# 64-column products in a delta-rule inversion on one Trainium2 core, with S5's skip moved from TensorE to VectorE

## The chip, the cores and the metric

The kernel runs on one core of a Trainium2 chip. The metric is the device time of one execution in microseconds (us). The core's engines work from queues of their own: TensorE (PE in the profile; its weight loads are PEld), VectorE (DVE), ScalarE (ACT), GpSimd (POOL) and SyncE (SP, which here issues most of the DMAs). All share the on-chip memory SBUF; TensorE writes its results to PSUM.

## The reference

A decoder trunk of two layers on 1024 positions with 1024 channels, all in f32. Each layer runs a token mixer beside a cross-attention into 256 memory tokens, projects both together, and ends with an MLP. The first layer's mixer is a gated delta rule with 8 heads of 128 channels in chunks, the second's is an S5 state-space layer. What matters here:

```python
def gated_delta_rule_chunked(q, k, v, g, beta):
    ...
    a_strict = jnp.where(strict, jnp.einsum('bhnid,bhnjd->bhnij', kb, k) * decay, 0.0)
    rhs = jnp.concatenate([vb, kb * jnp.exp(gc)[..., None]], axis=-1)
    sol = lax.linalg.triangular_solve(eye + a_strict, rhs, left_side=True, lower=True,
                                      unit_diagonal=True)
    ...

def s5_mixer(...):
    ...
    y = s5_scan(u, abar_re, abar_im, bbar_re, bbar_im, c_re, c_im)
    y = y + d_skip * u                         # the skip
    zg = jax.nn.gelu(y)
    out = zg * jax.nn.sigmoid(zg @ w_glu + b_glu)

for i in range(2):
    h = jnp.concatenate([mix, cross], axis=-1) @ w_o[i]
    x = layer_norm(DN_ALPHA * x + h, ln1_g[i], ln1_b[i])
    f = jnp.square(jax.nn.relu(x @ mlp_w1[i])) @ mlp_w2[i]
    x = layer_norm(DN_ALPHA * x + f, ln2_g[i], ln2_b[i])
```

## The kernel before

**Matmuls.** The large products split each f32 operand into a rounded high part and a rest in the type f32r, and add three products of 128x128 by 128x512 (`mm3`, L364 to L366). Small products are in plain f32; each of them appears on TensorE as two loads of weights and two matmul instructions. In a product the stationary operand (the first) is loaded as weights, the moving one (the second) streams past.

**The delta rule.** The kernel uses chunks of 128 positions, so a head has 8 tiles of 128x128, handled in two halves of four tiles. With N the negated strict part of a tile, it needs the inverse of I - N, transposed. It comes in steps. `gdn_keys_out` makes N^T of a half (tile `n`), writes its 32x32 diagonal blocks to DRAM (`ntd`), and then, in the kernel before, two masked copies of it (`ntf`): the blocks beside the diagonal at distance 32, and those at distance 64, each in a tile cleared by GpSimd, filled by ScalarE (L1040 to L1043) and written by a DMA that GpSimd issues. `gdn_inverse` inverts the 32x32 blocks of two heads at a time on VectorE and writes them to DRAM (`t32`, both ways round). `gdn_invert_tiles` grows them to 128x128 with five products of four tiles per half, all 128x128 by 128x128 on block-diagonal tiles in the kernel before. Every product goes to the one PSUM bank of the tag `pi`; VectorE adds the identity after two of the products (L1148), ScalarE copies the other three (L1153). That makes 8 heads x 2 halves x 5 = 80 products of four tiles. The 32x32 blocks are loaded by SyncE into two tiles that persist (`bds`), four loads for each; every other tile of the chain is a fresh one of the tag `h4` (six buffers) or, for the result, `h3` (seven).

`gdn_recur` is the recurrence over the eight tiles of a head and reads the results (`TT`). The order of the program is woven from generators: `gdn_fill` mixes the next head's projections with its inversion products, and `weave` mixes those with the recurrence of the head before.

**S5's matrices.** Beside the first MLP, `s5_side` makes the matrices of the second layer's mixer. `s5_mats`, called 16 times, has a group of four products `pz` of 128x16 by 128x128 (L1726). After each stands a product of 16x16 by 16x16 (L1727) which adds the skip: the identity times `dd`, a diagonal matrix of the skip's weights that VectorE makes (L1830). ScalarE copies the result to `z` (L1729), and GpSimd issues its DMA to DRAM (L1730).

**The order.** After the first weights are split, `settle` orders all instructions anew. It lists the instructions with their dependencies and buffers, gives each a price in us (`price`), and simulates the five engines, GpSimd's and SyncE's queues among them. TensorE takes its instructions roughly in the program's order (it may reach 40 us ahead), the other engines by the time at which TensorE will need their result, up to 70 us ahead. The order that comes out is fixed in the program; at run time each engine works through its own queue.

Of the kernel before, what the change touches and what calls it, by code (L numbers as in the profile page):

```python
# [10 lines left out]
F32 = mybir.dt.float32  # L11
F32R = mybir.dt.float32r
AF = mybir.ActivationFunctionType
ALU = mybir.AluOpType
AX = mybir.AxisListType

P = 128
# [13 lines left out]
class Trunk:  # L31
# [244 lines left out]
    def price(self, i, big):  # L276

        E = mybir.EngineType
        if i.opcode == "DMACopy":
# [8 lines left out]
            q = [x.bass_ap.ap for x in (i.ins[0], i.outs[0])]  # L288
# [3 lines left out]
        if i.engine == E.PE:  # L292
            if i.ins[0].dtype == F32R:
                return 0.014 + 0.416e-3 * big, 0.39 if big > 256 else 0.29, 0
            return (0.11, 0.27, 0) if i.is_transpose else (0.222, 0.39, 0)
        q = [x.bass_ap.ap[-1] for l in (i.ins, i.outs) for x in l if getattr(x, "bass_ap", None) is not None]
        slow = 1.65 if any(s > 1 and c > 1 for s, c in q) else 1.0
        scalars = any(math.prod(c for s, c in x.bass_ap.ap[1:]) == 1 for x in i.ins if getattr(x, "bass_ap", None) is not None) and big > 1
        if i.engine == E.Activation:
            bank = self.home.get(i.ins[0].bass_ap.tensor.name, "s")[0] == "ps"  # L300
            if i.opcode == "TensorCopy":
                t = (0.05 if bank else 0.096) + 0.84e-3 * big * slow
            else:
                t = (0.08 if bank else 0.125) + 0.8e-3 * big + (0.08 if len(i.outs) > 1 else 0.0) + (0.07 if scalars else 0.0)
            return t, t + 0.1, 0
        if i.engine == E.Pool:
            t = 0.02 + 0.87e-3 * big if i.opcode == "Memset" else 0.5 if big < 2 else 1.0 if big < 8 else 0.17 + 2.1e-3 * big
            return t, t + 0.05, 0
        wide = sum(c > 1 for x in i.ins if getattr(x, "bass_ap", None) is not None for c in [math.prod(c for s, c in x.bass_ap.ap[1:])])
# [507 lines left out]
    def gdn_consts(self):  # L817
        nc = self.nc
# [14 lines left out]
        self.early = [early[:, 2 * P + 64 * n:2 * P + 64 * (n + 1)].rearrange("p (t h) -> p t h", t=8) for n in range(2)]  # L833
        self.bds = [self.tile("h4", [P, 4, P], F32, "bd") for _ in range(2)]
        for o in self.bds:
            nc.gpsimd.memset(o, 0.0)
        cw = scr[:, P + 8 + 13 * 64:].rearrange("p (m j) -> p m j", j=4)
        nc.sync.dma_start(cw, self.a["cw"])
# [6 lines left out]
        self.ded = self.dp.tile([8, 2, P, 4, P], F32, tag="ded", name="ded")  # L845
        self.ntf = self.dp.tile([8, 2, 2, P, 4, P], F32, tag="ntf", name="ntf")
        self.ntd = self.dp.tile([8, 8, 4, 32, 32], F32, tag="ntd", name="ntd")
# [150 lines left out]
    def gdn_keys_out(self, h, hf):  # L998


        nc = self.nc
        V = nc.vector
# [34 lines left out]
        nc.gpsimd.dma_start(self.ntd[h, t4].rearrange("t b j i -> (b j) t i"), pkd)  # L1037
        for w, q in enumerate((32, 64)):
            nm = self.tile("h1", [P, 4, P], F32, "nm")
            nc.gpsimd.memset(nm, 0.0)  # L1040
            for b in range(0, P, 2 * q):
                nc.scalar.copy(nm[b:b + q, :, b + q:b + 2 * q], n[b:b + q, :, b + q:b + 2 * q])
            nc.gpsimd.dma_start(self.ntf[h, hf, w], nm)  # L1043

# [81 lines left out]

    def block_diag(self, h, hf, w):

        o = self.bds[w]
        for b in range(4):  # L1130
            q = slice(32 * b, 32 * b + 32)
            self.nc.sync.dma_start(o[q, :, q], self.t32[w, h, 4 * hf:4 * hf + 4, b].rearrange("t i c -> i t c"))
        return o

    def gdn_invert_tiles(self, h):

        nc = self.nc
        idb = self.ident.unsqueeze(1).to_broadcast([P, 4, P])

        def mm4(a, b):  # L1140
            ps = self.psum("pi", "iv", (P, 4, P))
            for t in range(4):
                nc.tensor.matmul(ps[:, t, :], a[:, t, :], b[:, t, :], start=True, stop=True)  # L1143
            return ps

        def plus_i(ps):
            o = self.tile("h4", [P, 4, P], F32, "zi")
            nc.vector.tensor_tensor(o, ps, idb, op=ALU.add)  # L1148
            return o

        def keep(ps, tag):
            o = self.tile(tag, [P, 4, P], F32, "iv")
            nc.scalar.copy(o, ps)  # L1153
            return o

        def masked(hf, w):
            o = self.tile("h4", [P, 4, P], F32, "nm")
            nc.sync.dma_start(o, self.ntf[h, hf, w])
            return o

        out = self.TT[h] = []
        for hf in range(2):
            nm = masked(hf, 0)
            T32, V32 = self.block_diag(h, hf, 0), self.block_diag(h, hf, 1)
            zi = plus_i(mm4(nm, T32))
            yield 0.8
            T64 = keep(mm4(V32, zi), "h4")
            yield 0.8
            V64 = keep(mm4(zi, V32), "h4")
            nm = masked(hf, 1)  # L1170
            yield 0.8
            zi = plus_i(mm4(nm, T64))
            yield 0.8
            out.append(keep(mm4(zi, V64), "h3"))
            yield 0.8

# [535 lines left out]
    def s5_mats(self, m, b, co, banks):  # L1712
# [12 lines left out]
        for g in range(4):  # L1725
            nc.tensor.matmul(flat(pz[:16, g]), co[:, 0, 4 * b + g, :], flat(h1[:, g]), start=True, stop=False)  # L1726
            nc.tensor.matmul(pz[:16, g, 0, :], self.ident[:16, :16], dd[:, g, :], start=False, stop=True)  # L1727
        z = self.tile("h5", [P, 4, 8, 16], F32, "z")[:16]
        nc.scalar.copy(z, pz[:16])  # L1729
        nc.gpsimd.dma_start(self.zd[m, :, gs, 112:], z.rearrange("p g e o -> p g (e o)"))  # L1730
# [522 lines left out]
```

## Time and profile before

| | |
|---|---|
| runs (us) | 2645.47, 2647.72, 2644.42; median 2645.47 |
| span of the profiled execution | 2639.3 us, granted TensorE clock 0.994 |
| the profiled execution's own time | not listed apart; the three runs lie 5.1 to 8.4 above the span |
| TensorE busy | 2571.1 us (97%), 12749 matmul instructions |
| VectorE, ScalarE, GpSimd busy | 1936.8 (73%), 1320.7 (50%), 355.0 us (13%) |
| inversion products (L1143) | 640 instructions, 184.8 to 678.5 us |
| S5's pz products and skips (L1726, L1727) | 128 and 128 instructions, 1079.6 to 1429.1 us |

In the profile's rows a group reads as line, engine, operation, output and inputs, shapes (weights as rows*columns, then partitions x elements) and count, then busy time in us, the mean in ns of one, and the idle time of the engine before it with what ended it. Timeline rows begin with the start and the length in us. A row of a stage gives its window, its length, then busy time and count of each engine (PE, PEld, DVE, ACT, POOL), the granted clock, the DMA share and the GB/s. Matmuls are pipelined: their lengths overlap, and their price is read from the distance of their starts.

### The profile page before, as it was taken

The page shows a single profiled execution, that of the slowest core. Times are in us where ns is not written, and L with a number is a line of the kernel's source. Part 1 is how long each engine was busy: PE and PEld are TensorE (multiplying, and loading weights), DVE is VectorE, ACT ScalarE, POOL GpSimd, SP SyncE. Part 2 cuts the span into 40 slices and gives each one's busy share as a digit, 9 for nine tenths or more (in the row PEclk, how much of TensorE's full clock was granted, in tenths as well). Part 3 has the DMA queues.
Part 4 walks back from the last instruction along what each step waited for, and adds up shares of the span by engine and source line. Part 5 has one row for each costly group of instructions (what it writes and reads, how often), then busy time and mean ns, then how long its engine had stood idle before and what let it go on. Part 6 is the DMA issues. An engine that isn't in the chain of part 4 may idle for free.

```text
span 2639.3 us, 37224 instructions
## 1 busy us (share of the span) xinstructions
PE 2571.1 (97%) x12749; PEld 2123.5 (80%) x12749; DVE 1936.8 (73%) x3560; ACT 1320.7 (50%) x2943; POOL 355.0 (13%) x509
## 2 busy tenths in 40 slices
PE   8999999999999999999999999999999999999998
PEld 6888788888887787777777888878887788888886
DVE  6674757566768798878988966673768766578778
ACT  6766566674526456544444344573235454454441
POOL 1211211120003003311110022212002000000002
PEclk9999999999999999999999999999999999999999
DMA  5443444444422556666444277755313444573432
GB/s 193 132 118 110 116 116 115 135 135 138 165 95 84 180 186 205 208 235 237 160 161 153 108 235 226 215 178 168 131 72 124 164 159 156 194 276 133 160 107 92
DMA packets 259630, 414.04 MB, mean 157 GB/s; under 512 B 96960, under 2 KB 113552, under 8 KB 259440
## 3 DMA queue, kind: packets, MB, share of 16 engines
q1 hardware_dynamic: 237808, 354.53, 40.4%
q0 software_dynamic: 19328, 52.94, 6.7%
q10 hardware_dynamic: 2304, 4.20, 0.4%
q8 instruction: 100, 1.64, 0.2%
q14 instruction: 90, 0.74, 0.1%
HBM read 279.97 MB, written 131.56 MB: 156 GB/s over the span
## 4 chain that ended last, share of the span: by engine, by line
PE 75%; DVE 9%; issue 6%; ACT 5%; DMA 3%; POOL 2%; SPq 0%; POOLq 0%; DVEq 0%; ACTq 0%
PE q L364 6%; PE q L365 6%; PE q L366 6%; PE tm L366 3%; PE tm L364 3%; PE tm L365 3%; PE pB L364 3%; PE pB L365 3%; PE pB L366 3%; PE iv L1143 2%; PE wi L364 2%; PE wi L365 2%; PE wi L366 2%; PE pC L364 2%; PE pC L366 2%
## 5 line engine op out<-in xcount | busy, mean ns | idle before, releaser
L364 PE MATMUL q<-wkh,hkh 128*128 128x512 f32 x784 | 306.7, 391 | 0.0
L365 PE MATMUL q<-wkl,hkh 128*128 128x512 f32 x784 | 306.0, 390 | 0.4 <-DVE wkl L775 0.4
L366 PE MATMUL q<-wkh,hkl 128*128 128x512 f32 x784 | 305.6, 390 | 0.0
L774 ACT CAST wkh<-wr 128x512 fp32r<-128x512 f32 x168 | 104.9, 624 | 236.0 <-PE q L365 188.2
L364 PEld LDWEIGHTS q<-wkh,hkh 128*128 128x128 f32 x784 | 147.2, 188 | 31.7 <-ACT wkh L774 0.5
L365 PEld LDWEIGHTS q<-wkl,hkh 128*128 128x128 f32 x784 | 147.2, 188 | 31.1 <-DVE wkl L775 1.1
L366 PEld LDWEIGHTS q<-wkh,hkl 128*128 128x128 f32 x784 | 147.2, 188 | 30.3
L775 DVE TENSOR_TENSOR wkl<-wr,wkh 128x512 fp32r<-128x512 f32 x168 | 115.7, 688 | 70.1 <-issue 53.3
L364 PE MATMUL wi<-xTh,wih 128*128 128x512 f32 x384 | 158.5, 413 | 0.0
L365 PE MATMUL wi<-xTl,wih 128*128 128x512 f32 x384 | 153.2, 399 | 0.0
L366 PE MATMUL wi<-xTh,wil 128*128 128x512 f32 x384 | 153.1, 399 | 0.0
L479 POOL TENSOR_SCALAR mv<-mv 128x1 f32<-128x1 f32 x32 | 24.8, 775 | 871.2 <-DVE mv L478 630.9
L775 DVE TENSOR_TENSOR hkl<-hr,hkh 128x512 fp32r<-128x512 f32 x196 | 134.1, 684 | 1.9 <-ACT hkh L774 1.9
L1522 DVE TENSOR_TENSOR y<-tm,y 128x512 f32<-128x512 f32 x128 | 88.0, 688 | 61.5 <-PE tm L366 59.8
L774 ACT CAST hkh<-hr 128x512 fp32r<-128x512 f32 x196 | 120.8, 616 | 0.0
L366 PEld LDWEIGHTS wi<-xTh,wil 128*128 128x128 f32 x384 | 72.8, 190 | 14.2
L364 PEld LDWEIGHTS wi<-xTh,wih 128*128 128x128 f32 x384 | 73.2, 191 | 12.6 <-issue 0.5
L365 PEld LDWEIGHTS wi<-xTl,wih 128*128 128x128 f32 x384 | 73.2, 191 | 12.4 <-issue 0.3
L768 DVE TENSOR_TENSOR y<-q,y 128x512 f32<-128x512 f32 x112 | 72.1, 682 | 0.0
L364 PE MATMUL tm<-ow,ok 128*128 128x512 f32 x160 | 63.3, 397 | 0.0
L365 PE MATMUL tm<-ow,ok 128*128 128x512 f32 x160 | 62.5, 391 | 0.0
L366 PE MATMUL tm<-ow,ok 128*128 128x512 f32 x160 | 62.4, 390 | 0.0
(541 smaller groups left out, 7589.2 us busy)
## 6 DMA issues: line engine op xcount, KB each, us to landing
hr<-hd SPq DMA_DIRECT2D x212, 256.0 KB, 2.6
wr<-in_w_dram SPq DMA_DIRECT2D x56, 512.0 KB, 4.8
hd<-u SPq DMA_DIRECT2D x92, 256.0 KB, 2.0
w1r<-in_w_dram SPq DMA_DIRECT2D x40, 512.0 KB, 3.8
w1r<-in_w_dram SPq DMA_DIRECT2D x64, 256.0 KB, 4.3
hd<-hid SPq DMA_DIRECT2D x60, 256.0 KB, 2.8
hd<-p SPq DMA_DIRECT2D x60, 256.0 KB, 2.6
wir<-in_w_in_dram SPq DMA_DIRECT2D x24, 512.0 KB, 3.4
```

The lines of the kernel that those rows point to most:

```text
L364: mm(ps, a[0], b[0], start=start, stop=False, skip_group_check=onto)
L365: mm(ps, a[0], b[1], start=False, stop=False, skip_group_check=onto)
L366: mm(ps, a[1], b[0], start=False, stop=stop, skip_group_check=onto)
L479: nc.gpsimd.tensor_scalar(mv[:, 2:3], mv[:, 1:2], 1e-5, None, op0=ALU.add)
L768: V.tensor_tensor(o, bank[t], o, op=ALU.add)
L774: nc.scalar.copy(hi, s)
L775: nc.vector.tensor_tensor(lo, s, f32(hi), op=ALU.subtract)
L1143: nc.tensor.matmul(ps[:, t, :], a[:, t, :], b[:, t, :], start=True, stop=True)
L1522: nc.vector.tensor_tensor(y[c], ps, y[c], op=ALU.add)
```

## The change

**N^T whole.** `gdn_keys_out` writes N^T as it is, once per half; the clears, the masked copies and one of the two stores go. `gdn_invert_tiles` loads from it the 64 and the 32 columns that it uses, in two DMAs.

**64 columns.** The five products stay, in the same order and number, but each has 64 stationary and 64 moving columns per tile and an output of 64 partitions. Their operands are pieces: `lead` (the inverses of blocks 0 and 2 beside each other), `unit` (identity blocks that stay, and the product's results copied between them), `pair` (two windows of 64 columns), the loaded N^T, and the result tile `TT`. The three first persist for the whole stage, are cleared once in `gdn_consts`, and hold three of the six buffers of `h4`. `TT` is a fresh tile of `h3`, opened at the start of the half, cleared by GpSimd, filled with the four 32x32 blocks by SyncE's DMAs and with results by ScalarE and VectorE. The copies out of PSUM get smaller: per half ScalarE makes two of 32x128 and three of 64x256, VectorE two of 32x128. Loads of 32x32 blocks go from eight to six per half.

**S5's skip.** The 64 products with the identity go; VectorE adds `dd` to the first of eight column blocks while it copies it, ScalarE copies the other seven.

**Prices.** `settle` prices an f32 product that is no transpose by its wider operand: 0.012 + 0.00164 us a column, which is 0.222 at 128 as before and 0.117 at 64. The generator of the inversion announces 0.5 us a product to the weaving where it announced 0.8.

```diff
--- before.py
+++ after.py
@@ -292,7 +292,10 @@
         if i.engine == E.PE:
             if i.ins[0].dtype == F32R:
                 return 0.014 + 0.416e-3 * big, 0.39 if big > 256 else 0.29, 0
-            return (0.11, 0.27, 0) if i.is_transpose else (0.222, 0.39, 0)
+            if i.is_transpose:
+                return 0.11, 0.27, 0
+            wide = max(math.prod(c for s, c in x.bass_ap.ap[1:]) for x in i.ins[:2])
+            return 0.012 + 1.64e-3 * wide, 0.39, 0
         q = [x.bass_ap.ap[-1] for l in (i.ins, i.outs) for x in l if getattr(x, "bass_ap", None) is not None]
         slow = 1.65 if any(s > 1 and c > 1 for s, c in q) else 1.0
         scalars = any(math.prod(c for s, c in x.bass_ap.ap[1:]) == 1 for x in i.ins if getattr(x, "bass_ap", None) is not None) and big > 1
@@ -831,9 +834,12 @@
         nc.gpsimd.affine_select(mn, mn, [[1, P]], ALU.is_ge, -1e30, base=0, channel_multiplier=-1)
         self.maskneg = mn
         self.early = [early[:, 2 * P + 64 * n:2 * P + 64 * (n + 1)].rearrange("p (t h) -> p t h", t=8) for n in range(2)]
-        self.bds = [self.tile("h4", [P, 4, P], F32, "bd") for _ in range(2)]
-        for o in self.bds:
+        self.lead, self.unit, self.pair = (self.tile("h4", [P, 4, P], F32, "bd") for _ in range(3))
+        for o in (self.lead, self.pair):
             nc.gpsimd.memset(o, 0.0)
+        nc.gpsimd.memset(self.unit, 0.0)
+        for r, c in ((0, 0), (32, 64), (64, 32)):
+            nc.scalar.copy(self.unit[r:r + 32, :, c:c + 32], self.ident[r:r + 32, r:r + 32].unsqueeze(1).to_broadcast([32, 4, 32]))
         cw = scr[:, P + 8 + 13 * 64:].rearrange("p (m j) -> p m j", j=4)
         nc.sync.dma_start(cw, self.a["cw"])
         self.cw = cw
@@ -843,7 +849,7 @@
         self.ng = ng
         self.kdd = self.dp.tile([8, 2, P, 4, P], F32, tag="kdd", name="kdd")
         self.ded = self.dp.tile([8, 2, P, 4, P], F32, tag="ded", name="ded")
-        self.ntf = self.dp.tile([8, 2, 2, P, 4, P], F32, tag="ntf", name="ntf")
+        self.ntf = self.dp.tile([8, 2, P, 4, P], F32, tag="ntf", name="ntf")
         self.ntd = self.dp.tile([8, 8, 4, 32, 32], F32, tag="ntd", name="ntd")
         self.t32 = self.dp.tile([2, 8, 8, 4, 32, 32], F32, tag="t32", name="t32")
 
@@ -1035,12 +1041,7 @@
             q = slice(32 * b, 32 * b + 32)
             nc.scalar.copy(pkd[q], n[q, :, q])
         nc.gpsimd.dma_start(self.ntd[h, t4].rearrange("t b j i -> (b j) t i"), pkd)
-        for w, q in enumerate((32, 64)):
-            nm = self.tile("h1", [P, 4, P], F32, "nm")
-            nc.gpsimd.memset(nm, 0.0)
-            for b in range(0, P, 2 * q):
-                nc.scalar.copy(nm[b:b + q, :, b + q:b + 2 * q], n[b:b + q, :, b + q:b + 2 * q])
-            nc.gpsimd.dma_start(self.ntf[h, hf, w], nm)
+        nc.gpsimd.dma_start(self.ntf[h, hf], n)
 
     def gdn_inverse(self, h0):
 
@@ -1124,55 +1125,53 @@
             nc.gpsimd.dma_start(dst[1][:, 8 * y:8 * y + 8, 16:32], Tt[q])
             nc.gpsimd.dma_start(dst[0][:, 16:32, 8 * y:8 * y + 8], Tn[q])
 
-    def block_diag(self, h, hf, w):
-
-        o = self.bds[w]
-        for b in range(4):
+    def blocks(self, o, h, hf, w, places):
+
+        for b, c in places:
             q = slice(32 * b, 32 * b + 32)
-            self.nc.sync.dma_start(o[q, :, q], self.t32[w, h, 4 * hf:4 * hf + 4, b].rearrange("t i c -> i t c"))
-        return o
+            self.nc.sync.dma_start(o[q, :, c:c + 32], self.t32[w, h, 4 * hf:4 * hf + 4, b].rearrange("t i c -> i t c"))
 
     def gdn_invert_tiles(self, h):
 
         nc = self.nc
-        idb = self.ident.unsqueeze(1).to_broadcast([P, 4, P])
+        V = nc.vector
+        T32, zi = self.lead, self.unit
+        B = self.pair.rearrange("p t (w c) -> p w t c", w=2)
+        A, B = B[:, 0], B[:, 1]
 
         def mm4(a, b):
-            ps = self.psum("pi", "iv", (P, 4, P))
+            ps = self.psum("pi", "iv", (P, 4, P))[:64, :, 0:64]
             for t in range(4):
-                nc.tensor.matmul(ps[:, t, :], a[:, t, :], b[:, t, :], start=True, stop=True)
+                nc.tensor.matmul(ps[:, t], a[:, t], b[:, t], start=True, stop=True)
             return ps
-
-        def plus_i(ps):
-            o = self.tile("h4", [P, 4, P], F32, "zi")
-            nc.vector.tensor_tensor(o, ps, idb, op=ALU.add)
-            return o
-
-        def keep(ps, tag):
-            o = self.tile(tag, [P, 4, P], F32, "iv")
-            nc.scalar.copy(o, ps)
-            return o
-
-        def masked(hf, w):
-            o = self.tile("h4", [P, 4, P], F32, "nm")
-            nc.sync.dma_start(o, self.ntf[h, hf, w])
-            return o
 
         out = self.TT[h] = []
         for hf in range(2):
-            nm = masked(hf, 0)
-            T32, V32 = self.block_diag(h, hf, 0), self.block_diag(h, hf, 1)
-            zi = plus_i(mm4(nm, T32))
-            yield 0.8
-            T64 = keep(mm4(V32, zi), "h4")
-            yield 0.8
-            V64 = keep(mm4(zi, V32), "h4")
-            nm = masked(hf, 1)
-            yield 0.8
-            zi = plus_i(mm4(nm, T64))
-            yield 0.8
-            out.append(keep(mm4(zi, V64), "h3"))
-            yield 0.8
+            NT = self.tile("h4", [P, 4, P], F32, "nt")
+            for o, c, w in ((0, 64, 64), (64, 32, 32)):
+                nc.sync.dma_start(NT[:, :, o:o + w], self.ntf[h, hf][:, :, c:c + w])
+            TT = self.tile("h3", [P, 4, P], F32, "iv")
+            nc.gpsimd.memset(TT, 0.0)
+            self.blocks(T32, h, hf, 0, ((0, 0), (2, 32)))
+            self.blocks(TT, h, hf, 1, ((0, 0), (1, 32), (2, 64), (3, 96)))
+            out.append(TT)
+            ps = mm4(NT[:, :, 32:96], T32[:, :, 0:64])
+            nc.scalar.copy(zi[32:64, :, 0:32], ps[32:64, :, 0:32])
+            V.tensor_copy(zi[96:128, :, 32:64], ps[0:32, :, 32:64])
+            yield 0.5
+            ps = mm4(TT[:, :, 0:64], zi.rearrange("p t (w c) -> p t w c", c=32)[:, :, 0:3:2])
+            nc.scalar.copy(A[0:64], ps)
+            yield 0.5
+            ps = mm4(zi[:, :, 0:64], TT.rearrange("p t (w c) -> p t w c", c=32)[:, :, 1:4:2])
+            nc.scalar.copy(TT[0:32, :, 32:64], ps[0:32, :, 0:32])
+            V.tensor_copy(TT[64:96, :, 96:128], ps[32:64, :, 32:64])
+            yield 0.5
+            ps = mm4(NT[:, :, 0:64], A)
+            nc.scalar.copy(B[64:128], ps)
+            yield 0.5
+            ps = mm4(B, TT[:, :, 64:128])
+            nc.scalar.copy(TT[0:64, :, 64:128], ps)
+            yield 0.5
 
     def gdn_queries_out(self, h, hf):
 
@@ -1723,10 +1722,10 @@
         dd = self.dd(8 * m + 4 * b)
         pz = self.psum(banks[0], "pz", (P, 4, 8, 16))
         for g in range(4):
-            nc.tensor.matmul(flat(pz[:16, g]), co[:, 0, 4 * b + g, :], flat(h1[:, g]), start=True, stop=False)
-            nc.tensor.matmul(pz[:16, g, 0, :], self.ident[:16, :16], dd[:, g, :], start=False, stop=True)
+            nc.tensor.matmul(flat(pz[:16, g]), co[:, 0, 4 * b + g, :], flat(h1[:, g]), start=True, stop=True)
         z = self.tile("h5", [P, 4, 8, 16], F32, "z")[:16]
-        nc.scalar.copy(z, pz[:16])
+        nc.scalar.copy(z[:, :, 1:8], pz[:16, :, 1:8])
+        V.tensor_tensor(z[:, :, 0], pz[:16, :, 0], dd, op=ALU.add)
         nc.gpsimd.dma_start(self.zd[m, :, gs, 112:], z.rearrange("p g e o -> p g (e o)"))
         g1 = self.combine(co[:, 0], co[:, 1], re[:, 0:8, gl], im[:, 0:8, gl], b, "G1T")
         pg = self.psum(banks[1], "pg", (P, 4, P))
```

## The prediction

> **What bounds the kernel now.** I read the page's engine shares first, then the busy time by stage, then the two groups of products that the change touches, line by line in the timeline.
>
> ```profile
> span 2639.3 us, 37224 instructions
> PE 2571.1 (97%) x12749; PEld 2123.5 (80%) x12749; DVE 1936.8 (73%) x3560; ACT 1320.7 (50%) x2943; POOL 355.0 (13%) x509
> PE 75%; DVE 9%; issue 6%; ACT 5%; DMA 3%; POOL 2%; SPq 0%; POOLq 0%; DVEq 0%; ACTq 0%
> 180.00:760.00 580.00, 569.66 (x3295) 490.69 (x3294) 374.60 (x703) 341.29 (x1069) 85.22 (x120) 0.99 0.44 130
> 1060.00:1440.00 380.00, 375.22 (x1776) 292.06 (x1775) 324.57 (x628) 170.28 (x299) 63.78 (x105) 1.00 0.56 194
> ```
>
> The reader is to see that TensorE is busy for 97% of the span and makes 75% of the chain that ended last. The fourth line is the delta rule's stage, from the first inversion product to the last heads: of 580 us TensorE is idle for 10, VectorE (374.60) and ScalarE (341.29) for over 200 each. The fifth is the stage in which S5's matrices are made beside the first MLP: TensorE is idle for 5 of 380 us at a granted clock of 1.00, VectorE is the next engine with 85%. So in both stages the change is worth what it takes from TensorE's queue, and not what it takes from the others.
>
> What one inversion product costs that queue is read from the starts, since the durations of pipelined matmuls overlap:
>
> ```profile
> 184.81 0.39 PE L364 MATMUL wi<-xTh,wih 128*128 128x512 f32 x1
> 185.04 1.05 PE L1143 MATMUL iv<-bd,nm 128*128 128x128 f32 x8
> 185.85 0.48 PE L365 MATMUL wi<-xTl,wih 128*128 128x512 f32 x1
> 186.16 0.40 PE L366 MATMUL wi<-xTh,wil 128*128 128x512 f32 x1
> L1143 PE MATMUL iv<-bd,nm 128*128 128x128 f32 x128 | 17.0, 275 | 0.0
> ```
>
> A projection matmul takes 0.23 (184.81 to 185.04). From 184.81 to 186.16 are 1.35 us with two of them, so a product of four tiles takes 1.35 - 0.46 = 0.89 us. Each tile's matmul is two instructions (x8 for four tiles), so an instruction takes 0.89 / 8 = 0.11. Each of the five forms has x128, which are 16 products of 8, so there are 80 products: 71 us.
>
> **Part 1, S5's skip.** A group of four products pz, each followed by its skip on the identity, looks like this (three more such pairs stand where lines are left out):
>
> ```profile
> 1375.30 0.39 PE L366 MATMUL q<-wkh,hkl 128*128 128x512 f32 x1
> 1375.62 0.39 PE L1726 MATMUL pz<-H,co 128*16 128x128 f32 x2
> 1375.94 0.21 PE L1727 MATMUL pz<-dd,ident 16*16 16x16 f32 x2
> ...
> 1377.47 0.50 PE L364 MATMUL q<-wkh,hkh 128*128 128x512 f32 x1
> 1377.80 0.39 PE L365 MATMUL q<-wkl,hkh 128*128 128x512 f32 x1
> ```
>
> From 1375.30 to 1377.80 are 2.50 us, less two matmuls of 0.23: the group costs 2.04, and 16 groups 32.6. What the group costs without the skips shows where a single product stands alone:
>
> ```profile
> 1079.31 0.40 PE L365 MATMUL pC<-xB,s1h 128*128 128x512 f32 x1
> 1079.64 0.11 PEld L1726 LDWEIGHTS pz<-H,co 128*16 128x16 f32 x2 [0.37 <-DVE H L1685]
> 1079.64 0.39 PE L1726 MATMUL pz<-H,co 128*16 128x128 f32 x2
> 1079.96 0.50 PE L364 MATMUL pA<-xB,a2h 128*128 128x512 f32 x1
> 1080.30 0.40 PE L365 MATMUL pA<-xB,a2h 128*128 128x512 f32 x1
> ```
>
> From 1079.31 to 1080.30 are 0.99 us, less 0.46: 0.53 for two instructions. Streaming takes 2 x 0.11 = 0.22 of that, by the instruction's price above. The other 0.31 are the change of shape: the weights are not loaded ahead, the first matmul starts 0.33 after the one before instead of 0.23, and the same happens on the way back, with the full load of weights in the open. Four products in a row pay this once: 0.53 + 6 x 0.11 = 1.19. The change saves 2.04 - 1.19 = 0.85 a group, **13.6 us** in 16. VectorE's add of 16x64 has its nearest row in the product that makes dd (below): 16 x 0.21 = 3.3 us on an engine that is idle for 55 us of this stage. ScalarE's copy gets shorter by an eighth. If that cover were gone, 3.3 us would come back.
>
> **Part 2, the inversion.** Both operands go from 128 to 64 columns. That both must is seen where only the moving one is narrow:
>
> ```profile
> 38.25 0.41 PE L929 MATMUL gc<-early 128*128 128x64 f32 x2
> 38.49 0.39 PE L930 MATMUL gl<-early 128*128 128x64 f32 x2
> 38.69 0.48 PE L366 MATMUL wi<-xTh,wil 128*128 128x512 f32 x1
> L1143 PEld LDWEIGHTS iv<-bd,nm x128: 186/192/193, 184.8 to 659.0; 128*128 128x128 f32 x128
> L1726 PEld LDWEIGHTS pz<-H,co x128: 92/93/97, 1079.6 to 1428.7; 128*16 128x16 f32 x128
> L1727 PE MATMUL pz<-dd,ident x128: 171/178/185, 1088.1 to 1429.1; 16*16 16x16 f32 x128
> ```
>
> Two instructions with 64 moving columns still take 0.20 to 0.24, because 128 columns of weights are loaded. A load grows by (192 - 93) / 112 = 0.9 ns a column. With 64 and 64 an instruction should take half of 0.11, 0.056; the floor is not above 0.04, since two skips of 16x16 last 0.21 together (1375.94) and 0.17 singly. So a product streams 8 x 0.056 = 0.45 us. Now comes the choice that decides this part: does a product with 64 stationary columns pay the 0.31 of the 16-column ones? The trace has no f32 matmul with 64 stationary columns. The ends are 0.08 (what the 128-column product pays: 185.85 to 186.16 is 0.31 instead of 0.23) and 0.31 + 48 x 0.0009 = 0.35. I take 0.35: the 16-column row is the only one in which stationary columns of an f32 product are fewer than the array's, and it shows the full price even without the skips beside it. Then a product costs 0.45 + 0.35 = 0.80 instead of 0.89, and 80 save 7.2 us.
>
> [...]
>
> A product is also sometimes cut in two by a step of the recurrence:
>
> ```profile
> 253.22 0.39 PE L1143 MATMUL iv<-zi,bd 128*128 128x128 f32 x2
> 253.45 0.39 PE L1295 MATMUL ks<-S,kT 128*128 128x128 f32 x2
> 253.67 0.39 PE L1298 MATMUL po<-S,gb 128*128 128x128 f32 x2
> 253.89 0.83 PE L1143 MATMUL iv<-zi,bd 128*128 128x128 f32 x6
> ```
>
> This is free today (0.22 between f32 matmuls throughout) and would cost a second 0.35. I estimate a cut for every twelfth product, 7 x 0.35 = 2.5 us. **The inversion nets 7.2 - 2.5 = 4.7 us.**
>
> **What the other engines lose.**
>
> ```profile
> L1153 ACT COPY iv<-iv 128x512 f32<-128x512 f32 x48 | 28.2, 587 | 32.5 <-PE iv L1143 32.1
> L1148 DVE TENSOR_TENSOR zi<-iv,ident 128x512 f32<-128x512 f32 x32 | 22.1, 690 | 24.4 <-PE iv L1143 24.3
> L1042 ACT COPY nm<-NT 32x128 f32<-32x128 f32 x32 | 9.3, 292 | 0.3
> L1042 ACT COPY nm<-NT 64x256 f32<-64x256 f32 x16 | 6.4, 403 | 0.3
> L1830 DVE TENSOR_TENSOR dd<-ident,dsk 16x64 f32<-16x64 f32 x16 | 3.3, 207 | 1.6 <-DMA h1d<-H 1.6
> PE kk L1031 <- ACT kd L1021: 4.7, 2, 2.9
> ```
>
> ScalarE drops the 15.7 us of L1042 and gets, by the sizes of L1042, 0.4 for each of three 64x256 and 0.29 for each of two 32x128 in a half, 1.8 x 16 = 28.6 us against the 28.2 of L1153; VectorE pays 2 x 0.29 x 16 = 9 us instead of 22.1. GpSimd does half as many clears of a whole tile (one per half, of the result tile, instead of two), and issues 16 stores of N^T instead of 32; SyncE issues two loads of N^T and six of blocks per half, where it issued two and eight, on its queue. All of this lies beside a TensorE that idles 10 of 580 us, so I count nothing; the most that it could give back is the kk wait, 4.7. The start is free too: one more clear on GpSimd and three small copies of the identity on ScalarE come before TensorE's first matmul, which waits for data:
>
> ```profile
> 8.54 0.13 PEld L882 LDWEIGHTS ba<-xTh,wbah 128*32 128x32 f32 x1 [8.54 <-ACT xTh L863]
> ```
>
> **The sum.** 13.6 + 4.7 = 18.3 us off the profiled span of 2639.3, to 2621.0. The times list does not say which of the runs was profiled; the median of the three, 2645.47, lies 6.2 above the span, and I keep that distance: 2645.5 - 18.3 = **2627 us**. A measurement of this kernel can tell about 0.2% (5.3 us) from no change.
>
> **The rivals.**
>
> *No change of shape is paid at 64 columns.* Then a product costs 0.45 + 0.08 = 0.53, 80 save 28.8, cuts are free, and the time is 2645.5 - 13.6 - 28.8 = 2603. For it: the f32r products with 16 and 32 stationary columns at the start follow each other without a visible cost. Against it: the f32 rows above. Chance 0.13.
>
> *GpSimd's queue holds the loads back (slower).* The result tile is now cleared on GpSimd, its blocks are loaded into it by SyncE after the clear, and behind those loads on SyncE's queue stand the projection weights. GpSimd's queue has long waits (us in all, times, longest):
>
> ```profile
> POOL t L1094 <- issue: 78.0, 4, 22.6
> ```
>
> One load of projection weights covers 48 x 0.23 = 11 us of TensorE (eight steps of three matmuls, for two halves of the positions). A clear caught behind the 22.6 us wait would starve TensorE for some 11.5 us; four times make 46, and the time 2627 + 46 = 2673. It decides from 18.3 / 4 = 4.6 us lost each of the four times. Against it: the order is planned with such queues in view, and loads are issued long ahead. Chance 0.08.
>
> *Narrow passes don't run faster (slower).* If an instruction with 64 columns keeps the 0.11 of the wide one, a product costs 0.89 + 0.35 = 1.24, 80 lose 28, cuts 2.5, S5 gives 13.6: 2645.5 + 28 + 2.5 - 13.6 = 2662. Against it stands the skip of 16x16 at 0.04. Chance 0.05. [...]
>
> *The cut comes back as waits.* The whole order after the first weights is planned anew from changed prices, and TensorE's idle time shifts; with the 18.3 lost in new idle time the result is 2645. TensorE's idle time of 68 us (2639.3 - 2571.1) is the place to look. Chance 0.07.
>
> **How the numbers follow.** My forecast of 2627 has the remaining 0.67; its own spread is 2617 to 2640 (idle time shifted by some 5 us either way, the S5 part between 10 and 17, the inversion between a loss of 2 and a gain of 9). The range reaches down to the first rival and up to no change: 2600 to 2646. Faster: 0.67 and 0.13, less a little for the forecast's upper end, 0.79. Same: 0.08. Slower: the two slow rivals, 0.13.
>
> **What would show it.** In the changed profile: TensorE's instructions fewer by 128 (the skips); a pz group of x8 with some 1.2 us from the matmul before to the matmul after it, less the usual spacing; an inversion product as x8 of 128*64, 128x64, starting 0.33 after the matmul before, some 0.45 long inside, and the next wide matmul with its load in the open; TensorE busy time lower and its idle time near 68. I am wrong if the entry is 0.23 (first rival), if the starts within a product lie 0.11 apart, if the loads of blocks wait for GpSimd while TensorE stands, or if the stage from 1060 us on does not shrink by 10 us or more.

## The result, and the profile after

The kernel after takes **2620.99 us** (median of four runs, 2618.05 to 2623.03) where the kernel before took 2644.94 beside it (four runs). The ratio is 0.9914 with an interval of 0.9899 to 0.9929: 24.0 us less, of which the interval allows 18.8 to 26.7. The forecast was 2627, in a range of 2600 to 2646, with a saving of 18.3: the direction and the range held, and the saving was some 6 us too small.

The profiled execution of after took 2622.83 us, 1.7 above its span. Its page begins like this (span, busy time by engine, shares of the chain that ended last):

```profile
span 2621.1 us, 36895 instructions
PE 2553.5 (97%) x12621; PEld 2092.7 (80%) x12621; DVE 1929.3 (74%) x3576; ACT 1304.3 (50%) x2930; POOL 338.1 (13%) x478
PE 78%; DVE 10%; issue 4%; ACT 3%; DMA 2%; POOL 2%; SPq 0%; DVEq 0%; POOLq 0%; ACTq 0%
```

TensorE has 128 instructions fewer and is busy for 17.6 us less; its idle time is 67.6 us where it was 68.2. The kernel is bound as before. To see where the time went, I cut both traces at two marks of TensorE's order, the first product of the MLP (`pA`) and the first product after S5's matrices (`wu`), and asked for the three stretches. The columns are the window, its length, busy time and count of PE, PEld, DVE, ACT and POOL, granted clock, DMA share and GB/s. Before:

```profile
0.00:822.60 822.60, 798.33 (x4452) 678.75 (x4452) 543.13 (x1062) 484.38 (x1449) 121.39 (x185) 0.99 0.43 129
822.60:1525.50 702.90, 688.14 (x3188) 545.34 (x3187) 613.42 (x1206) 336.24 (x604) 121.89 (x199) 1.00 0.52 179
1525.50:2639.30 1113.80, 1084.64 (x5113) 899.37 (x5111) 780.26 (x1294) 500.08 (x891) 111.67 (x126) 0.99 0.49 164
```

After:

```profile
0.00:813.40 813.40, 791.03 (x4452) 649.21 (x4453) 534.10 (x1062) 470.14 (x1436) 105.53 (x154) 0.99 0.40 118
813.40:1505.40 692.00, 674.88 (x3059) 541.81 (x3058) 614.82 (x1222) 334.44 (x604) 121.14 (x199) 1.00 0.54 181
1505.40:2621.10 1115.70, 1087.56 (x5113) 901.71 (x5111) 780.36 (x1294) 499.68 (x891) 111.47 (x126) 0.99 0.49 164
```

The delta stage is 9.2 us shorter (TensorE busy 7.3 less, idle 1.9 less), S5's stage 10.9 (busy 13.3 less, idle 2.4 more), and the last stage, which the change doesn't touch, 1.9 longer. That is 18.2 between these two executions, beside a forecast of 18.3; the nearness is partly luck. An execution is its span plus 1.7, so the profiled one of before took some 2641, 3.9 under its median, and that of after lies 1.8 over its own. The medians' 24.0 is the figure to explain.

One inversion product and one group of pz in the timeline of after (start, length):

```profile
188.02 0.39 PE L369 MATMUL wi<-xTh,wil 128*128 128x512 f32 x1
188.34 0.68 PE L1145 MATMUL iv<-iv,bd 128*64 128x64 f32 x8
188.95 0.50 PE L367 MATMUL wi<-xTh,wih 128*128 128x512 f32 x1
189.28 0.39 PE L368 MATMUL wi<-xTl,wih 128*128 128x512 f32 x1
188.34 0.54 PEld L1145 LDWEIGHTS iv<-iv,bd 128*64 128x64 f32 x8 [0.35 <-issue]
...
1358.77 0.39 PE L369 MATMUL q<-wkh,hkl 128*128 128x512 f32 x1
1359.09 1.05 PE L1725 MATMUL pz<-H,co 128*16 128x128 f32 x8
1360.06 0.50 PE L367 MATMUL q<-wkh,hkh 128*128 128x512 f32 x1
1360.40 0.40 PE L368 MATMUL q<-wkl,hkh 128*128 128x512 f32 x1
```

From 188.02 to 189.28 are 1.26 us, less two matmuls of 0.23: the product costs **0.80**, as forecast. It is entered 0.32 after the matmul before it, streams for 0.61, and is left 0.33 after the wide matmul that follows. The pz group costs 1360.40 - 1358.77 - 0.46 = **1.17** (forecast 1.19). Below, "slots" is the sum of this reading over all such groups in a trace, worked out from the starts of TensorE's instructions. The inversion's slots went from 72.8 us (80 products with 7 cuts, 87 groups) to 68.8 (11 cuts, 91 groups), 4.0 less. Those of pz and skips went from 33.8 to 19.3, 14.5 less.

So slots explain 18.5 of 24.0. The rest, 5.5 us, is within what the interval leaves open (18.8 at the least), but measuring the two parts one by one shows that it isn't spread evenly.

### The profile page after: what moved, and what is told of

Its sections match the earlier page's. It is cut to its first block, busy times and chain, and to the rows that moved or that the text cites. A ratio compares the mean times of both kernels' runs of the same rounds, so it can differ in the third digit from the quotient of the medians.

```text
span 2621.1 us, 36895 instructions
## 1 busy us (share of the span) xinstructions
PE 2553.5 (97%) x12621; PEld 2092.7 (80%) x12621; DVE 1929.3 (74%) x3576; ACT 1304.3 (50%) x2930; POOL 338.1 (13%) x478
## 4 chain that ended last, share of the span: by engine, by line
PE 78%; DVE 10%; issue 4%; ACT 3%; DMA 2%; POOL 2%; SPq 0%; DVEq 0%; POOLq 0%; ACTq 0%
PE q L367 6%; PE q L368 6%; PE q L369 6%; PE tm L367 3%; PE tm L369 3%; PE tm L368 3%; PE pB L367 3%; PE pB L368 3%; PE pB L369 3%; PE wi L367 3%; PE wi L368 2%; PE wi L369 2%; PE pC L367 2%; PE pC L369 2%; PE pC L368 2%
## 5 line engine op out<-in xcount | busy, mean ns | idle before, releaser
L367 PEld LDWEIGHTS wi<-xTh,wih 128*128 128x128 f32 x384 | 72.8, 190 | 16.7 <-ACT qT L975 3.1
L369 PEld LDWEIGHTS wi<-xTh,wil 128*128 128x128 f32 x384 | 72.8, 190 | 14.2
```

The lines of the kernel that those rows point to most:

```text
L367: mm(ps, a[0], b[0], start=start, stop=False, skip_group_check=onto)
L369: mm(ps, a[1], b[0], start=False, stop=stop, skip_group_check=onto)
```

## The experiments

Theory: TensorE's slots make the change; a product with 64 stationary columns pays the change of shape; what the other engines lose counts nothing. Rivals: the relief of the other engines counts; the plan of the order shifted by accident; the two parts don't add up.

**Each part alone.** The kernel before with the new skip:

```diff
--- before
+++ skip_alone
-            nc.tensor.matmul(flat(pz[:16, g]), co[:, 0, 4 * b + g, :], flat(h1[:, g]), start=True, stop=False)
-            nc.tensor.matmul(pz[:16, g, 0, :], self.ident[:16, :16], dd[:, g, :], start=False, stop=True)
+            nc.tensor.matmul(flat(pz[:16, g]), co[:, 0, 4 * b + g, :], flat(h1[:, g]), start=True, stop=True)
...
-        nc.scalar.copy(z, pz[:16])
+        nc.scalar.copy(z[:, :, 1:8], pz[:16, :, 1:8])
+        V.tensor_tensor(z[:, :, 0], pz[:16, :, 0], dd, op=ALU.add)
```

> The kernel before with S5's skip alone moved to VectorE; the inversion and its prices stay. If the time follows TensorE's slots, a pz group costs 1.17 us instead of 2.04 and 16 groups take 13.9 us off: 2631, with the delta rule's stage unchanged to 1 us. If part of it comes back as waits in the stage beside the first MLP (the changed kernel shortened that stage by 10.8 us, not 13.9), the gain is about 11 us: 2634.

Measured: 2633.96 beside 2644.48, ratio 0.9956 (0.9943 to 0.9969): 10.5 us less, with the 13.6 of the forecast inside the interval (8.2 to 15.1). Its slots fell by the 14.5 seen in after, and its second stage by 13.0 (702.9 to 689.9); the first and third were 1.3 and 2.0 longer.

The kernel after with the old skip (the same lines turned back):

```diff
--- after
+++ inv_alone
+            nc.tensor.matmul(pz[:16, g, 0, :], self.ident[:16, :16], dd[:, g, :], start=False, stop=True)
...
+        nc.scalar.copy(z, pz[:16])
```

> The changed kernel with S5's skip put back on TensorE: the 64-column inversion, N^T whole and the new prices remain. TensorE's slots alone (0.80 instead of 0.89 us a product, 11 cuts at 0.35) give 7.2 - 3.9 = 3 us: 2642. If the relief of the other engines and the shifted order matter too, as the 9.2 us by which the delta rule's stage got shorter suggest, it is 9 us: 2636. If the pieces cost waits, it is at or above 2645.

Measured: 2630.74, ratio 0.9949 (0.9938 to 0.9961): 13.7 us less (10.3 to 16.4), where 4.7 was forecast. The two parts add up (10.5 + 13.7 = 24.2), so this is where the missing us are: the inversion's part is worth almost three times its forecast, and its slots alone (4.0) don't pay for that.

Two readings tell where to look. Before and inv_alone begin their pages with TensorE busy for 2571.1 and 2562.0 us:

```profile
span 2629.0 us, 37124 instructions
PE 2562.0 (97%) x12749; PEld 2092.5 (80%) x12749; DVE 1927.8 (73%) x3560; ACT 1305.2 (50%) x2930; POOL 338.2 (13%) x478
```

Of the 10.3 us between these two spans 9.1 are busy time and only 1.2 are idle time (68.2 to 67.0), so waits that went away are the smaller part. And the granted clock, listed for each execution, averages 0.996 over the five of inv_alone and 0.994 over the eleven of before beside them: 0.002 of 2640 us, by estimate up to 5 us of the 13.7. The prediction has no term for the clock. How much of this belongs to the change and how much to the order that was planned for it, the runs below tell only in part.

**128 stationary columns again.** Everything of after, but each inversion product loads its whole tile as weights (64 columns move as in after, N^T is loaded whole, and the results are read from other partitions):

```diff
--- after
+++ wide_stationary
-            for o, c, w in ((0, 64, 64), (64, 32, 32)):
+            for o, c, w in ((0, 64, 64), (64, 0, 64)):
...
-            ps = mm4(NT[:, :, 32:96], T32[:, :, 0:64])
+            ps = mm4(NT, T32[:, :, 0:64])
...
-            ps = mm4(B, TT[:, :, 64:128])
-            nc.scalar.copy(TT[0:64, :, 64:128], ps)
+            ps = mm4(self.pair, TT[:, :, 64:128])
+            nc.scalar.copy(TT[0:64, :, 64:128], ps[64:128])
```

> The changed kernel with 128 stationary columns in the inversion's products (whole tiles as weights, N^T loaded whole); 64 moving columns, the pieces, the small copies and S5's part stay. If 64 stationary columns pay a change of shape, a product now enters at 0.23 instead of 0.33, lasts 8 x 0.11 inside and costs 0.89 instead of 0.80, and cuts become free: 80 x 0.09 - 3.9 = 3 us slower than the changed kernel, 2624. If there were no such price and the entry of 0.33 had another cause (the wait for the copies), the entry stays at 0.33, a product costs some 1.1 and the time is 2645. If the inversion's gain comes from the other engines' relief alone, the time equals the changed kernel's, 2621.

Measured: 2634.30, ratio 0.9962 (0.9950 to 0.9974), 13.3 above after, far from the 2624 expected. A product looks like this in its timeline:

```profile
183.80 0.40 PE L367 MATMUL wi<-xTh,wih 128*128 128x512 f32 x1
184.03 1.00 PE L1145 MATMUL iv<-bd,nt 128*128 128x64 f32 x8
184.84 0.47 PE L368 MATMUL wi<-xTl,wih 128*128 128x512 f32 x1
185.15 0.39 PE L369 MATMUL wi<-xTh,wil 128*128 128x512 f32 x1
```

The entry is 0.23 and not 0.32, and the inside is 0.81 (184.03 to 184.84) as with 128 moving columns in before (185.04 to 185.85). It goes by the stationary columns here; one load of weights takes 192 ns in the median, in after 138. The slots sum to 75.0, 6.2 above after. The first stage (0 to `pA`) shows what else was lost:

```profile
0.00:824.20 824.20, 798.62 (x4451) 679.85 (x4452) 533.44 (x1062) 471.61 (x1436) 105.19 (x154) 0.99 0.41 118
```

It is 10.8 us longer than in after: 7.6 of TensorE's busy time and 3.2 of idle time. This kernel has neither the masked copies nor VectorE's wide adds (DVE 533.44, POOL 105.19, as after), and yet it is no faster than skip_alone, which has them all (2634.0; its first stage takes 823.9). So with 128 columns the relief of the other engines shows no gain. It is no clean comparison: the slots of wide_stationary are 2.2 above those of before (75.0 and 72.8), its pieces and its order are others, and a relief of some 2 us could hide behind that.

**The masked copies back.** After, which still makes both masked copies on GpSimd and ScalarE and stores them unread, 15.7 us of ScalarE and 32 clears and 32 stores of GpSimd:

```diff
--- after
+++ masked_kept
...
+        for w, q in enumerate((32, 64)):
+            nm = self.tile("h1", [P, 4, P], F32, "nm")
+            nc.gpsimd.memset(nm, 0.0)
+            for b in range(0, P, 2 * q):
+                nc.scalar.copy(nm[b:b + q, :, b + q:b + 2 * q], n[b:b + q, :, b + q:b + 2 * q])
+            nc.gpsimd.dma_start(self.ntx[h, hf, w], nm)
```

> The changed kernel which also still makes the two masked copies of N^T, on GpSimd and ScalarE, and stores them where nobody reads them. If the work taken from ScalarE and GpSimd is hidden, as predicted, the time stays at 2621, within 2 us. If the 5 us by which the delta rule's stage got shorter beyond the products' own 4 us came from this relief, it is 2626.

Measured: 2636.65, ratio 0.9967 (0.9955 to 0.9979), 15.7 above after. Here the copies cost all that the inversion's part had won. The slots are about those of after (68.2); the first stage is 17.5 us longer, of which 14.9 are idle time of TensorE:

```profile
0.00:830.90 830.90, 793.59 (x4452) 650.53 (x4453) 534.24 (x1062) 487.03 (x1484) 140.35 (x218) 0.99 0.43 126
```

What TensorE waited for longest in this kernel, beside its start (engine, line, who released it, us in all, times, longest):

```profile
PE pe L1307 <- DVE R L1303: 6.4, 2, 6.1
PE ks L1301 <- DVE S L1318: 5.5, 1, 5.5
```

Neither wait is among the longest of after. The timeline of masked_kept at the second of them:

```profile
573.03 0.69 DVE L1039 SCALAR_TENSOR_TENSOR NT<-kk,D 128x512 f32<-128x512 f32 x1 [2.98 <-ACT D L1031]
573.64 0.34 DVE L1318 SCALAR_TENSOR_TENSOR S<-S,scr,pS 128x128 f32<-128x128 f32 x1
574.03 0.80 PE L1301 MATMUL ks<-S,kT 128*128 128x128 f32 x2 [5.47 <-DVE S L1318]
575.26 0.77 POOL L1044 DMA_DIRECT2D ntd<-pkd  x1 [0.70 <-ACT pkd L1043]
```

The recurrence's state S, for which TensorE stands still, is queued on VectorE behind the last head's N^T. That tile waits for its D; its kk products were done at 528. In after the same two instructions stand 43 us earlier:

```profile
529.75 0.69 DVE L1038 SCALAR_TENSOR_TENSOR NT<-kk,D 128x512 f32<-128x512 f32 x1 [1.02 <-ACT D L1030]
532.25 0.80 POOL L1043 DMA_DIRECT2D ntd<-pkd  x1 [2.61 <-ACT pkd L1042]
```

With these blocks late, the last reduction of the last inverse (`X<-pr`) starts on VectorE at 627 instead of 591, and the wait of 6.1 us on R ends at 628, where the recurrence again stands behind that work.

But this isn't the old work. Right ahead of the late tile's D, ScalarE's queue has the copies of the half before it:

```profile
568.63 1.01 ACT L1050 COPY nm<-NT 32x128 f32<-32x128 f32 x3
...
569.75 1.07 POOL L1051 DMA_DIRECT2D ntx<-nm  x2 [34.04 <-ACT nm L1050]
...
571.72 1.27 ACT L1031 ACTIVATE D<-D,scr 128x128 f32<-128x128 f32 x4
```

Their tiles were cleared by 536, and GpSimd waits 34 us for them. ScalarE isn't full: it idles 3.1 us before 564.5 and 2.4 before 568.1. Their place is the plan's: `settle` orders ScalarE's work by the time at which TensorE needs the result, and nothing reads `ntx`, so no product asks for these copies. (This is read from the program; no run gave them a reader.) In the kernel before, the inversion's products use them. There, and in skip_alone, the last `ntd` is sent at 551.3 and 552.6, not at 575.3, and the last reduction starts at 600 and 601. So masked_kept shows what copies cost that come late, and not what the old copies cost.

**Is it the plan?** The order is planned anew for every kernel, so two runs change the plan alone. In `price`, a 64-column matmul is priced at 0.20, near its slot (0.80 for four) instead of 0.117; in `yield8` the generator announces 0.8 us a product as before; `masked_price` and `masked_yield8` add the masked copies to these.

```diff
--- after
+++ price
-            return 0.012 + 1.64e-3 * wide, 0.39, 0
+            return (0.012 + 1.64e-3 * wide if wide > 64 else 0.2), 0.39, 0
--- after
+++ yield8 (at five places)
-            yield 0.5
+            yield 0.8
```

> The changed kernel with one number of the planner changed: a matmul with 64 columns is priced at 0.20 us, a quarter of what a product of four takes on the chip, instead of 0.117. Same instructions, another order. If the 5 us beyond the products' slots are the order's accident, this moves the time by some us either way (2616 to 2626) while a product's slot stays at 0.80. If the order plays no part, 2621 within 1 us.

> The changed kernel whose inversion generator announces 0.8 us a product to the weaving, as before, instead of 0.5. Same instructions, another order. The products' slots stay at 68.8 us in all; the time shows how far an order alone moves it: 2621 within 6 us, the difference in waits and in the clock's loss and not in slots.

> Masked copies kept as before, and the 64-column matmul priced at 0.20: the fourth corner beside the changed kernel (2621), the other price (2627) and the kept copies (2636.6, with two waits of 5.5 and 6.1 us in which the recurrence stands behind other work on VectorE). If ScalarE's and GpSimd's relief is worth the 15 us by itself, this is 2627 + 15 = 2642. If the two waits are accidents of that one order, it is within some 4 us of 2627, with no wait over 4 us in the delta rule's stage.

> Masked copies kept, with the 0.8 of the run beside it. If the relief is worth 15 us by itself, 15 us above the run beside it. If the stalls were an accident of one order, within some 4 us of it.

| kernel | us | ratio | cuts | last `ntd` sent at |
|---|---|---|---|---|
| before | 2644.94 | 1 | 7 | 551.3 |
| skip_alone | 2633.96 | 0.9956 | 7 | 552.6 |
| after | 2620.99 | 0.9914 (0.9899 to 0.9929) | 11 | 532.3 |
| yield8 | 2619.93 | 0.9903 (0.9890 to 0.9917) | 7 | 531.6 |
| price | 2627.04 | 0.9929 (0.9916 to 0.9943) | 16 | 537.0 |
| masked_kept | 2636.65 | 0.9967 (0.9955 to 0.9979) | 7 | 575.3 |
| masked_price | 2636.42 | 0.9967 (0.9955 to 0.9978) | 13 | 577.7 |
| masked_yield8 | 2637.20 | 0.9967 (0.9955 to 0.9979) | 7 | 574.4 |

The plan alone may move the time: with the truer price the median is 6.0 above after, 4 by the ratios, whose intervals overlap; five more cuts are some 1.7 of that (5 x 0.34). That order's 2627.04 is what the prediction forecast for the change. With the copies the three orders come to 2636 or 2637, which is 15.7, 9.4 and 17.3 above the kernel beside each, with the late blocks and the same kind of wait. For masked_price neither expectation holds: 2636.4 lies between the 2642 of a relief worth 15 us by itself and the 2631 at most of an accident. The rows of masked_price and of masked_yield8:

```profile
PE ks L1301 <- DVE S L1318: 12.8, 3, 6.8
...
PE ks L1301 <- DVE S L1318: 12.5, 2, 6.8
```

So the stall isn't an accident of one order. But all three orders share the copies that nobody reads, and in all three GpSimd waits 34 us or more for them (34.0, 34.7, 34.2). What stays open is what the old copies, read as they were, would cost beside 64 columns: no run has them. masked_kept also has one more store, and its N^T is read by the copies as well as by the store, so the tile lives longer. That the tiles of `h1` run out behind it is likely but was not tried; nor were ScalarE's, GpSimd's and the buffers' shares taken apart.

**The price of the shape.** If a change of shape costs 0.3 us, a product made wider than it need be is faster. The pz product reads 16 columns of `co`; here it loads 128 (the output's first 16 rows are used):

```diff
--- after
+++ wide_pz
-            nc.tensor.matmul(flat(pz[:16, g]), co[:, 0, 4 * b + g, :], flat(h1[:, g]), start=True, stop=True)
+            c = 16 * (4 * b + g)
+            nc.tensor.matmul(flat(pz[:, g]), co.rearrange("p a g o -> p (a g o)")[:, c:c + P], flat(h1[:, g]), start=True, stop=True)
```

> The changed kernel with pz's 16 stationary columns widened to 128 (the columns that follow in the same tile; only the first 16 output rows are used). More columns, so slower if the load of weights were the price: the load goes from 93 to 190 ns. If the change of shape is the price, a group enters at 0.23 instead of 0.32, runs 8 x 0.11, and costs 0.89 instead of 1.17: 16 x 0.28 = 4.5 us faster than the changed kernel, 2616.5. If neither, 2621.

Measured: 2616.61, ratio 0.9900 (0.9886 to 0.9914), 4.4 below after; the intervals of the two ratios overlap, so the slots are the firmer evidence, and they fell by 4.1, from 19.3 to 15.2. In its timeline:

```profile
1353.29 0.39 PE L369 MATMUL q<-wkh,hkl 128*128 128x512 f32 x1
1353.51 1.05 PE L1726 MATMUL pz<-H,co 128*128 128x128 f32 x8
1354.32 0.48 PE L367 MATMUL q<-wkh,hkh 128*128 128x512 f32 x1
1354.64 0.40 PE L368 MATMUL q<-wkl,hkh 128*128 128x512 f32 x1
```

Eight times the columns, and the group costs 1.35 - 0.46 = 0.89 instead of 1.17: the entry is 0.22 instead of 0.32, the inside 0.81 instead of 0.97, and the next start behind it comes 0.32 later instead of 0.34. So the price of these groups is one of shape, most of it on entry and inside, and not one of size.

**Fewer entries.** The price is per group, so groups were joined: the third and fourth product of a half, and the fifth of the first half with the first of the second, share a bank and follow each other.

```diff
--- after
+++ paired
+            ps = bank()
+            mm(ps[:, 0], zi[:, :, 0:64], windows(TT, slice(1, 4, 2)))
+            mm(ps[:, 1], NT[:, :, 0:64], A)
...
+            mm(ps[:, 0], B, TT[:, :, 64:128])
+            if hf == 0:
+                mm(ps[:, 1], NT[:, :, 32:96], T32[:, :, 0:64])
```

> The changed kernel with products of the inversion put back to back: the third and the fourth product (which do not need each other) in one group of 16 instructions and one PSUM bank, and the fifth product of a head's first half with the first product of its second half. A head has 7 groups instead of 10. A group's change of shape is 0.09 on entry, 0.105 on the way out and 0.14 inside (0.608 less 8 x 0.058), 0.34 together, so 24 groups fewer save 8 us: 2613. If the price belonged to the matmuls and not to the change of shape, nothing is saved: 2621. If the longer groups hold up the recurrence, it is slower than 2621.

Measured: 2618.44, ratio 0.9899 (0.9887 to 0.9912), 2.6 below after. The slots fell by 9.0 (68.8 to 59.8, 64 groups), and the first stage by 7.5; then the second stage gave 5.0 back (697.0 instead of 692.0), with a wait that after does not have:

```profile
1450.85 0.76 PE L367 MATMUL tm<-w2h,hk 128*128 128x512 f32 x1 [4.32 <-DVE y L771]
```

Both edits together (`paired_wide_pz`), and the wide pz with only the third and fourth product joined (`p34_wide_pz`, without the join across the halves):

> The paired products together with the widened pz. If both only remove changes of shape on TensorE's queue, the gains add: 8 + 4.5 us below the changed kernel, 2608.5. If one of them only shifted waits, less: 2612 to 2616.

> The widened pz with only the third and the fourth product in one group: 16 groups fewer than the changed kernel. TensorE's slots are 4.1 us (pz) and 16 x 0.34 = 5.4 us below the changed kernel's: 2611.5 if no new wait appears, up to 2617 if some of it comes back as waits, as 4 of 9 us did where the products were paired twice.

Measured: 2615.44, ratio 0.9888 (0.9874 to 0.9902), and 2614.99, ratio 0.9881 (0.9867 to 0.9895). The page of the last:

```profile
span 2613.4 us, 36898 instructions
PE 2540.4 (97%) x12621; PEld 2091.2 (80%) x12621; DVE 1928.8 (74%) x3576; ACT 1306.3 (50%) x2930; POOL 337.9 (13%) x478
```

It beats both kernels: 30.5 us under the one before, 6.0 under the one after, with 13.1 us less of TensorE's busy time than after. Of its 6.0, the wide pz alone gave 4.4; of the joined products' 6.0 of slots 1.6 are left between the medians, and idle time is 73.0 where after has 67.6 and wide_pz 70.6, so they are hardly worth having here.

## Why the prediction was right, and where it fell short

- **Part 1, the skip: right.** 2.04 to 1.17 a group (forecast 1.19), 14.5 of slots in all (13.6), 10.5 us by itself with 13.6 inside the interval. VectorE's adds cost it the 3.3 us that were forecast, and in skip_alone TensorE idles 0.9 us more in this stage than before (15.7 and 14.8), so most of them hide:

```profile
L1728 DVE TENSOR_TENSOR z<-pz,dd 16x64 f32<-16x64 f32 x16 | 3.3, 205 | 0.0
```

- **Part 2, the product: right.** 0.80 as forecast. The choice that decided it, that 64 stationary columns pay the 16-column price, is shown by the entry of 0.32 and, the other way round, by the entries of wide_stationary and wide_pz, 0.23 and 0.22. The inside takes 0.61 and not the forecast 0.45: of the 0.34 beyond the streaming (instructions 0.058 apart), 0.09 are paid before the product, 0.14 inside and 0.10 behind it. The rows show this for f32 with 64 and 16 stationary columns; the f32r products with 16 and 32 columns at the start pay nothing visible (0.23 apart in before from 13.3 us on).
- **Cuts: 11, not 7.** Slots of the inversion fell by 4.0 (forecast 4.7). A small miss, and `price` and `yield8` show that the plan sets it (16 and 7).
- **The step that fell short: "All of this lies beside a TensorE that idles 10 of 580 us, so I count nothing."** The inversion's part measured 13.7 (10.3 to 16.4) and not 4.7, with slots near their forecast, so the rest of its sum was too small. It has no term for the granted clock, to which up to 5 us point (0.996 and 0.994), and none for the order, which `price` moves by some 4 to 6 us with the same instructions. Its bound for what relief could give back, the kk wait of 4.7, only went to 2.7. How much the relief of ScalarE and GpSimd is worth stays open: late, unread copies cost 9 to 17 us, through S and R on VectorE's queue, but that isn't the old kernel's work.
- **Luck in the total.** Part 1 came out 3.1 below its forecast and part 2 9.0 above, so the sum is nearer to its forecast than the larger part is.
- **Span and median.** The 6.2 kept between them was larger than the 1.7 of any one execution; it stood for the profiled execution being a fast one of its kernel. That cost nothing here, since the medians were compared in the end.
- **The rivals.** *No change of shape* and *narrow passes don't run faster* fell by the rows of one product (inside, 0.61 for eight instructions, 0.076 for each and 0.058 between most of their starts). *GpSimd's queue* fell: POOL's work went from 355.0 to 338.1 us and among the waits of its matmuls in after none is for a load of blocks. *The cut comes back as waits* did not come for this change, but it is just what happened to paired and to p34_wide_pz.

## What to carry to other kernels

Price a narrow product by its shape before its columns: here a group between wide matmuls paid some 0.3 us beyond its streaming (0.34 at 64 stationary columns), four products of 64 columns saved a tenth (0.80 instead of 0.89), and 16 columns loaded as 128 took 0.89 instead of 1.17. To price work that a change removes, put it back together with its reader: a planner that orders by need can place unread work late, and what waits behind it then measures the plan. And where an order is planned by machine, a few us either way can belong to the plan, so a gain of that size wants more than one order, and a look at the granted clock of each.

## What was not expected of the hardware

In masked_kept a short stall cost TensorE more than its own length. After the wait on S the granted clock (third column from the right) is down:

```profile
570.00:574.00 4.00, 0.00 (x0) 0.00 (x0) 0.99 (x3) 3.24 (x12) 1.35 (x3) 0.82 0.49 174
574.00:576.00 2.00, 1.97 (x7) 1.78 (x8) 0.35 (x1) 1.53 (x6) 1.28 (x2) 0.50 0.92 320
576.00:580.00 4.00, 4.00 (x16) 3.44 (x15) 1.30 (x2) 2.42 (x5) 1.38 (x5) 0.57 0.39 148
...
629.00:633.00 4.00, 3.58 (x11) 3.00 (x11) 3.62 (x6) 1.19 (x3) 2.29 (x3) 0.50 0.67 153
```

The clock is 0.50 from 574 to 576 and in most of the 4 us behind; in such stretches of before and after wide matmuls start 0.43 apart instead of 0.23. In those two traces the stretches are 3.41 us long or two or three times that (the one at each program's end aside), and at 0.50 each costs at most half its length. The first stage of after holds three of them, 10.2 us; in masked_kept the waits on S and R bring some 6.8 us each, by the clock of the windows around them. A wait of 5.5 us should be booked as some 8 (an estimate from these rows: 5.5, and 1.0 + 1.7 lost in the second and third).

It doesn't take a long wait. In after, TensorE is busy for 1.93 of the 3.41 us before 597.03, and the longest of its idle pieces there is 0.8:

```profile
593.62:597.03 3.41, 1.93 (x9) 1.01 (x9) 2.94 (x8) 1.05 (x3) 3.32 (x5) 1.00 0.87 239
597.03:600.44 3.41, 3.41 (x15) 3.02 (x14) 1.85 (x3) 1.82 (x7) 0.65 (x2) 0.50 0.61 207
600.44:604.00 3.56, 3.56 (x22) 3.10 (x21) 2.36 (x6) 1.99 (x7) 0.00 (x0) 1.00 0.39 99
```

Counted on the grid of 3.41 us on which these stretches start in before and after (the first 30 and the last 20 us left out): all nine stretches at the full clock with 2.0 us of idle time or more were followed by half the clock, of the seven with 1.48 to 1.70 two were (1.48 and 1.67, both in after), and none with less. So in after 1.5 us of idle time in pieces were enough, and a kernel at 97% still meets it.
